# Expert weights into the slot that falls free next, the first pair's rows by gather, scaled rows stored by GpSimd

## The chip, the cores and the metric

One Trainium2 chip; the kernel runs on 1 core of it. The metric is the device time of one execution in microseconds (us). A core has TensorE (PE; its weight loads are listed apart as PEld), VectorE (DVE), ScalarE (ACT), GpSimd (POOL) and SyncE (SP), which here only issues DMAs; 16 DMA engines move the data.

## The reference

One encoder block on 512 tokens of 1024 features, float32. First a mixer (a bidirectional recurrence and a windowed attention, gated and projected), whose result is added to x; then a mixture of experts, the part this case is about, cut from the reference:

```python
g_sel = jnp.argmax(g_logits, axis=-1)
e_in_group = jnp.take_along_axis(e_logits, g_sel[:, None, None], axis=1)[:, 0]
top_val, top_idx = lax.top_k(e_in_group, TOP_K_IN_GROUP)
weights = p_group * jax.nn.softmax(top_val, axis=-1)
...
for e in range(N_EXPERTS):
    he = jax.nn.silu(ht @ w_gate_e[e]) * (ht @ w_up_e[e])
    y = y + combine[:, e:e + 1] * (he @ w_down_e[e])
```

Every token goes to 2 of 32 experts, two of the eight of its group. An expert has a gate and an up matrix of 1024 x 256 and a down matrix of 256 x 1024. The input of the experts is RMSNorm(x1) with the gain `norm2_g`, x1 being the mixer's result.

## The kernel before, in words

The mixer takes the first 630 us or so. What the change touches begins with `out_rows`: the last projection of the mixer gives x1 in four row tiles of 128 tokens, in two column halves. For each of the eight blocks `post` adds x, stores it to the output, transposes it for the router's logits, and lets GpSimd multiply it by the gain `g2` into a tile `r_xg` (two buffers), which SP stores to `h2` in DRAM. `route` then finds each token's two experts on VectorE (one-hot rows `E`, their sum `ES`), counts places with TensorE (`pp`), and builds a list of 64 slots per expert: `pos`, then `r_P`, then 16 small matmuls into the bank `list`, then `idx` (row numbers) for the gathers. The weights of the list (`r_tw`, `r_Pf`, `wgt`, `wts`) and `eid`, for the rare overflow, follow with low priority.

The experts are worked in pairs: pair p is the experts p and p + 16, 64 slots each, side by side on TensorE's columns. For pair 0 the rows are not gathered: `first_x` builds them before `idx` is known, as a product of x1 with a one-hot matrix `r_oh`, in two halves of 16 matmuls (two trace rows each), scaled by `g8` on the way out. For the pairs 1 to 15, `gather` fetches the rows from `h2` by an indirect DMA on GpSimd's queue into one of two tiles `xe`, and `expert_x` transposes them on TensorE into `xT`. `gate_up` is G: 16 matmuls per pair, the first half with the matrices j = 0 of both experts, the second with j = 1. `down` is Y (tile `Yd`), the down product; `finish` scatters it with an add into the output. The loop runs G of pair p, with a piece of the down work of pair p - 1 in its middle, then the transposes of pair p + 1, then Y of pair p - 1. So TensorE is done with the down matrices of pair p - 1 after the gate/up matrices of pair p.

Weights: 96 loads of 1 MB in the order of `USE`: per pair four gate/up pieces (in_wgu) and two down matrices (in_wd). There are 23 slots (`NSLOT`). Load i goes to slot i for i under 23, and then to the slot that load i - 23 had. All loads are issued by SP, which works its queue in order and stands where a slot isn't free. Slots 0 to 14 open during `out_gated` and `out_rows`; slots 15 to 22 lie where the tiles of the output projection and of `route` were (pools `opw`, `op`, and the raw weights), and are free when these are done. In the order of `USE` load 6p + n belongs to pair p; n = 0 to 3 are gate/up, 4 and 5 down.

Of the kernel before, what the change touches and what calls it, by code (L numbers as in the profile page):

```python
# [8 lines left out]
F32 = mybir.dt.float32  # L9
# [3 lines left out]
AF = mybir.ActivationFunctionType  # L13
OP = mybir.AluOpType
# [158 lines left out]


USE = [(p, j, e2) for p in range(16) for j in range(3) for e2 in range(2)]


class K:
# [797 lines left out]
    def out_rows(self):  # L976

        nc, op, zT = self.nc, self.op, self.zT
        x1 = self.x1 = []

        op.tile([P, 4, P], F32, name="x1T", tag="x1T", bufs=2)
        for tt in range(4):
            x1.append(op.tile([P, D], F32, name="x1_%d" % tt))
            nc.sync.dma_start(x1[-1], self.A["x"][tt * P:(tt + 1) * P])
        rl = self.bank("lg", [P, 4, 36], 1)
        ss = op.tile([P, 2, 4], F32, name="r_ss")

        def post(n, tt, ps):

            x = x1[tt][:, n * T:(n + 1) * T]  # L990
            self.tt(x, ps, x, OP.add)
            sl = slice(tt * P, (tt + 1) * P), slice(n * T, (n + 1) * T)
            nc.sync.dma_start(self.A["out"][sl], x)
            self.act(ps, x, AF.Square, scale=1.0 / 32, accum_out=ss[:, n, tt:tt + 1])
            if n + tt == 0:

                self.act(op.tile([P, 1], F32, name="r_tab"), ss[:, 0, 0:1], AF.Sqrt)
            pt = self.bank("mm", [P, 4, P], 4) if n == 1 and tt >= 2 else self.bank("tp", [P, 4, P], 2)
            for k in range(4):
                self.tr(pt[:, k], x[:, k * P:(k + 1) * P])  # L1000
            xT = op.tile([P, 4, P], F32, name="x1T", tag="x1T", bufs=2)
            if n == 1 and tt == 3:
                nc.vector.tensor_copy(xT[:, 0:2], pt[:, 0:2])
                self.act(xT[:, 2:4], pt[:, 2:4])
            elif tt % 2 == 1:
                self.act(xT, pt)
            else:
                nc.vector.tensor_copy(xT, pt)
            for k in range(4):
                self.mm(rl[:, tt], xT[:, k], self.wr[:, 4 * n + k], start=(n + tt + k == 0), stop=(n == 1 and tt + k == 6),  # L1010
                        skip_group_check=True)
            xg = op.tile([P, T], F32, name="r_xg", tag="r_xg", bufs=2)
            self.tt(xg, x, self.g2[:, sl[1]], eng=nc.gpsimd)
            nc.sync.dma_start(self.h2[sl], xg)

        for n in range(2):
            ps = [self.bank("mm", [P, T], 4) for tt in range(4)]
            w = {}
            for m2 in range(4):
                with self.low(-LOW):  # L1020
                    hi, lo = [w_.rearrange("p (a k) b -> p a (k b)", a=2) for w_ in self.wload(4 * n + m2, "w_out")]
                for i in range(2):
                    w[2 * m2 + i] = hi[:, i], lo[:, i]

                ms = [2 * m2, 2 * m2 + 1] if n == 0 or m2 < 2 else range(4, 8) if m2 == 3 else []
                steps = [(m, tt) for m in ms for tt in range(4)]
                for m, tt in sorted(steps, key=lambda u: u[::-1]) if len(ms) == 4 else steps:
                    sl = slice(tt * P, (tt + 1) * P)
                    self.mm3(ps[tt], tuple(t[:, m % 4, sl] for t in zT[m // 4]), w[m], m == 0, m == 7)
                    if m == 7 and tt >= LAG:  # L1030
                        post(n, tt - LAG, ps[tt - LAG])
                self.load_upto(min(NS1 + NS2, NL1 + (NS1 + NS2 - NL1) * (4 * n + m2 + 1) // NL2))
            for tt in range(4 - LAG, 4):
                post(n, tt, ps[tt])
        st = self.st
        self.stt(st, ss[:, 0], 1e-6, ss[:, 1], OP.add, OP.add)
        self.act(st, st, AF.Sqrt)
        nc.vector.reciprocal(st, st)
        lg = op.tile([P, 4, 36], F32, name="r_lg")
        self.tt(lg, rl, st[:, :, None].to_broadcast([P, 4, 36]))  # L1040
        self.tt(lg, lg, self.br[:, None].to_broadcast([P, 4, 36]), OP.add)
        self.route(lg)


    def route_setup(self):
# [9 lines left out]
        nc.sync.dma_start(self.br, bc(self.A["br"], 0, 36))  # L1055
        self.g2 = op.tile([P, D], F32, name="g2")
        nc.sync.dma_start(self.g2, bc(self.A["norm2_g"], 0, D))
        self.g8 = self.rt.tile([P, 8], F32, name="g8")
        nc.sync.dma_start(self.g8, self.A["norm2_g"].rearrange("o (p k) -> p (o k)", p=P))
        self.h2 = self.dram.tile([T, D], F32, name="h2")  # L1060
        rt = self.rt

# [9 lines left out]
    def route(self, lg):  # L1072
# [33 lines left out]
        self.mm(pp, self.tri, ES, start=True, stop=False, skip_group_check=True)  # L1106
        for j in range(3):
            self.mm(pp[:, j + 1:], self.one, bc(ES[:, j, None], 3 - j, 32), start=False, stop=(j == 2), skip_group_check=True)

        m = t1("r_m", 4, 2)  # L1110
        self.stt(m, ES[:, :, ::16], 1e6, pp[:, :, ::16], OP.mult, OP.add)
        oh = self.op.tile([P, 8, 64], F32, name="r_oh", tag="r_xg", bufs=2)
        ready = nc.vector.scalar_tensor_tensor(oh, self.cs("iota")[:, None, :].to_broadcast([P, 8, 64]), 1e6,
                                               m.rearrange("p t h -> p (t h)")[:, :, None].to_broadcast([P, 8, 64]), op0=OP.add, op1=OP.is_equal)
        oh = oh.rearrange("p (t h) s -> p t (h s)", t=4)
        self.first_x(oh, 0)
        tw = self.op.tile([P, 2, 4, 32], F16, name="r_tt")
        self.tt(tw, E, bc(self.cs("tok")[:, None, :, None], 2, 4, 32))
        pos = self.pos
        sc = t3("r_sc")  # L1120
        self.tt(sc, E, bc(pp[:, None], 2, 4, 32))
        with self.tc.issue_after(ready.ins):
            nc.vector.tensor_reduce(pos, sc, axis=V, op=OP.add)
        Pm = self.op.tile([P, 2, 4, 64], F16, name="r_P", tag="x1T", bufs=2)
        self.tt(Pm, bc(self.cs("iota")[:, None, None, :], 2, 4, 64), bc(pos[:, :, :, None], 2, 4, 64), OP.is_equal)
        kt = [(k, i) for k in range(2) for i in range(4)]
        for k, i in kt:
            for h in range(2):
# [1 line left out]
                        stop=(k + i == 4), skip_group_check=True)  # L1130
        self.idx = self.rt.tile([P, 16], I32, name="idx")
        self.slots(self.idx, self.lps[:, 0, :16])
        self.first_x(oh, 1)

        with self.low(), self.tc.issue_after(ready.ins):
            Pf = self.op.tile([P, 2, 4, 64], F32, name="r_Pf", tag="r_xg", bufs=2)
# [22 lines left out]
            sc = self.op.tile([P, 2, 4, 32], F32, name="r_es", tag="r_xg", bufs=2)  # L1159
            self.tt(sc, E, bc(self.cs("iota")[:, None, None, :32], 2, 4, 32))  # L1160
            nc.vector.tensor_reduce(self.eid, sc, axis=V, op=OP.add)

    def first_x(self, oh, hf):

        ps = self.bank("mm", [P, 4, P], 4)
        for k in range(4):
            for tt in range(4):
                self.mm(ps[:, k], self.x1[tt][:, hf * 4 + k:D:8], oh[:, tt], start=(tt == 0), stop=(tt == 3), skip_group_check=True)
        for k in range(4):
            o, g = self.xT[0][:, 4 * hf + k], self.g8[:, 4 * hf + k:4 * hf + k + 1]  # L1170
            if k % 2:
                self.act(o, ps[:, k], AF.Copy, scale=g)
            else:
                self.ts(o, ps[:, k], g)

    def slots(self, idx, ps):

# [93 lines left out]
    def load_upto(self, n):  # L1271

        while self.loaded < min(n, 96):
            p, j, e2 = USE[self.loaded]
            i = self.loaded
            self.slot.append(i if i < NSLOT else self.slot[i - NSLOT])
            self.loaded += 1
            if p == 15 and j == 2:

                for h in range(2 * e2):  # L1280
                    for k in range(2):
                        self.load(i - 1 + k, p, j, k, h)
            else:
                self.load(i, p, j, e2)
# [64 lines left out]
    def moe(self):  # L1349
# [5 lines left out]
            return bass.IndirectOffsetOnAxis(ap=idx, axis=0)  # L1355

        def gather(p):
            xe = xb[(p - 1) % NX]
            if p <= NX:
                nc.gpsimd.memset(xe, 0.0)  # L1360
            nc.gpsimd.indirect_dma_start(out=xe, out_offset=None, in_=self.h2[:, :], in_offset=rows(self.idx[:, p:p + 1]),
                                         bounds_check=T - 1, oob_is_err=False)
            return xe

        def mat(p, j, e2):
            return self.wslot[self.slot[USE.index((p, j, e2))]]
# [4 lines left out]
            self.load_upto(6 * (p + 1) + 4 + NSLOT)  # L1371
            self.scatter(y, self.idx[:, p:p + 1])

        xe = [gather(p) for p in range(1, NX)]
        xT = self.xT[0]
        self.xT.append(self.mo.tile([P, 8, P], F32, name="xT1"))
        self.xn = 0
        for p in range(16):
            if p + NX < 16:
                xe.append(gather(p + NX))  # L1380
            if p == 15:

                for _ in late:
                    pass
                late = None
            sg = self.gate_up([[mat(p, j, e2) for j in range(2)] for e2 in range(2)], xT, self.wts[:, 1, p:p + 1], late)
            if p == 1:
                tasks = self.tasks()
            if p in (1, 4):
                next(tasks)  # L1390
            if p < 15:
                xT = self.expert_x(xe.pop(0))
            for _ in late or ():
                pass
            late = finish(p, sg)
# [75 lines left out]
```

## Time and profile before

| | |
|---|---|
| median of 3 runs | 943.88 us (940.36 to 944.55) |
| the profiled execution | 947.55 us |
| its span, first to last instruction | 945.4 us |
| mean granted TensorE clock | 0.959 |
| PE busy | 829.0 us, 88% of the span |
| PEld busy | 540.2 us, 57% |
| DVE busy | 433.2 us, 46% |
| ACT busy | 309.4 us, 33% |
| POOL busy | 175.8 us, 19% |
| loads of gate/up pieces by SP, issue to landing | 64, median 20.9 us |
| gathers by POOL, issue to landing | 15, median 9.0 us |

Busy shares are means over stages with different limits. The expert part, from some 694 us to the end, is a quarter of the span; what a change there is worth is read from its own stretches and waits. A DMA's issue on SP is shown as a short instruction; when its bytes arrive is its landing. The DMA share is the mean busy share of the 16 DMA engines.

### The profile page before, as it was taken

The numbers are of one execution on the slowest core, as the hardware profiler recorded it, in microseconds if no ns is written. First come the engines' busy times: TensorE is split into PE (matmuls) and PEld (weight loads), VectorE is DVE, ScalarE is ACT, GpSimd is POOL, SyncE is SP. The second block draws the span as 40 slices with busy tenths as digits, with TensorE's granted clock in tenths as the row PEclk, the third lists the DMA queues.
The fourth block names the chain that finished last, engine by engine and source line by source line (L and its number), as shares of the span: only waits on it lengthen the run. The fifth ranks groups of instructions, "written<-read, shape, count | busy, mean of one in ns | idle before, by whom it ended". The sixth has DMA issues, their size and how long they took to land. (4 is left out here: it accounts for less than half of the span.)

```text
span 945.4 us, 17389 instructions
## 1 busy us (share of the span) xinstructions
PE 829.0 (88%) x7248; PEld 540.2 (57%) x7248; DVE 433.2 (46%) x875; ACT 309.4 (33%) x670; POOL 175.8 (19%) x152
## 2 busy tenths in 40 slices
PE   8999887889988987699998999999799998888884
PEld 7676655656666655466666678778653333332221
DVE  5699884565689588124347306632512111111010
ACT  6444531213443553135647522232211111111110
POOL 2611121120003132132313220012111222111101
PEclk9999896999998998699999999999799999999998
DMA  6321131121122322321314648889976999999992
GB/s 220 102 64 38 35 100 37 55 68 57 46 69 77 103 68 68 116 84 59 112 47 139 201 140 317 282 313 364 362 310 245 389 365 394 393 395 404 402 354 49
DMA packets 49775, 175.96 MB, mean 186 GB/s; under 512 B 7639, under 2 KB 14423, under 8 KB 37664
## 3 DMA queue, kind: packets, MB, share of 16 engines
q1 hardware_dynamic: 45232, 166.66, 48.0%
q0 software_dynamic: 4464, 8.18, 3.5%
q8 instruction: 57, 0.93, 0.4%
q14 instruction: 22, 0.18, 0.1%
HBM read 158.78 MB, written 24.12 MB: 193 GB/s over the span
## 5 line engine op out<-in xcount | busy, mean ns | idle before, releaser
L199 PE MATMUL G<-ws,xT 128*64 128x512 f32 x512 | 129.5, 596 | 8.8 <-DMA ws<-in_wgu 5.6
L199 PE MATMUL mm<-hT_hi,w_lo 128*128 128x512 f32 x264 | 114.2, 433 | 7.9 <-ACT oth L184 6.8
L187 POOL TENSOR_TENSOR w_lo<-w_raw,w_hi 128x1024 fp32r<-128x1024 f32 x29 | 70.7, 2438 | 242.9 <-ACT w_hi L184 242.9
L199 PE MATMUL mm<-hT_hi,w_hi 128*128 128x512 f32 x264 | 112.2, 425 | 0.0
L199 PE MATMUL mm<-hT_lo,w_hi 128*128 128x512 f32 x264 | 111.9, 424 | 0.0
L199 PEld LDWEIGHTS G<-ws,xT 128*64 128x64 f32 x512 | 42.8, 137 | 84.3 <-issue 64.4
L199 PE MATMUL Yd<-ws,hT 128*64 128x512 f32 x256 | 67.1, 607 | 10.5 <-ACT y L184 9.4
L184 ACT ACTIVATE w_hi<-w_raw 128x1024 fp32r<-128x1024 f32 x59 | 62.2, 1054 | 28.1 <-PE mm L199 27.9
L199 PEld LDWEIGHTS mm<-hT_hi,w_lo 128*128 128x128 f32 x264 | 52.1, 197 | 25.9 <-issue 14.9
L187 DVE TENSOR_TENSOR w_lo<-w_raw,w_hi 128x1024 fp32r<-128x1024 f32 x30 | 37.1, 1236 | 50.5 <-ACT w_hi L184 50.5
L199 PEld LDWEIGHTS mm<-hT_lo,w_hi 128*128 128x128 f32 x264 | 52.0, 197 | 12.6 <-issue 2.0
L199 PEld LDWEIGHTS mm<-hT_hi,w_hi 128*128 128x128 f32 x264 | 52.2, 198 | 11.5 <-issue 1.7
L187 DVE TENSOR_TENSOR sg<-sg,G 128x256 f32<-128x256 f32 x16 | 6.7, 420 | 100.1 <-ACT sg L184 100.0
L1401 POOL DMA_INDIRECT out<-y,idx x16 | 25.2, 1578 | 127.2 <-DVE y L194 83.1
L194 DVE TENSOR_SCALAR y<-Yd,wts 128x512 f32<-128x512 f32 (+1 forms) x16 | 11.7, 734 | 79.3 <-PE Yd L199 64.8
L184 ACT ACTIVATE sg<-G,wts 128x256 f32<-128x256 f32 x16 | 7.6, 474 | 121.2 <-PE G L199 121.2
L199 PE MATMUL c<-R,T 128*32 128x64 f32 (+1 forms) x992 | 36.3, 231 | 8.2 <-DVE R L647 2.6
L647 DVE COPY R<-c 32x128 f32<-32x128 f32 x64 | 18.8, 293 | 54.0 <-ACT R L184 53.3
L199 PEld LDWEIGHTS Yd<-ws,hT 128*64 128x64 f32 x256 | 17.1, 136 | 45.2 <-ACT y L184 22.4
L199 PE MATMUL tp<-T,KB 64*64 64x128 f32 x512 | 35.6, 284 | 7.4 <-ACT T L184 7.1
L199 PEld LDWEIGHTS c<-R,T 128*32 128x32 f32 (+1 forms) x992 | 26.2, 125 | 27.5 <-issue 13.9
L184 ACT ACTIVATE T<-tp 64x256 f32<-64x256 f32 x64 | 23.9, 377 | 46.1 <-DVE T L187 45.2
(318 smaller groups left out, 1493.0 us busy)
## 6 DMA issues: line engine op xcount, KB each, us to landing
ws<-in_wgu SPq DMA_DIRECT2D x64, 1024.0 KB, 20.9
ws<-in_wd SPq DMA_DIRECT2D x30, 1024.0 KB, 22.3
w_raw<-in_w_in SPq DMA_DIRECT2D x43, 512.0 KB, 3.6
d_oth<-oth SPq DMA_DIRECT2D x16, 256.0 KB, 2.0
w_raw<-in_wo SPq DMA_DIRECT2D x8, 512.0 KB, 4.1
w_raw<-in_w_out SPq DMA_DIRECT2D x8, 512.0 KB, 5.0
x_in<-in_x SPq DMA_DIRECT2D x4, 512.0 KB, 4.8
ga<-d_oth SPq DMA_DIRECT2D x8, 256.0 KB, 5.3
```

What stands on the lines that cost most here:

```text
L184: self.nc.scalar.activation(out, in_, func, **kw)
L187: (eng or self.nc.vector).tensor_tensor(out, a, b, op=op)
L194: self.nc.vector.tensor_scalar(out, a, s1, None, op0=op0)
L199: return self.nc.tensor.matmul(out, l, r, start=start, stop=stop, **kw)
L647: self.nc.vector.tensor_copy(R[u, :, blk, p2], ps[u, 2:4])
L1401: self.nc.gpsimd.indirect_dma_start(out=self.A["out"], out_offset=bass.IndirectOffsetOnAxis(ap=idx, axis=0), in_=y, in_offset=None, bounds ...
```

## The change

Three edits. First, the slot of load i from 23 on is that of the load whose matrix TensorE finishes next, by a table `FREE`: the four gate/up pieces of pair p, then the two down matrices of pair p - 1. Second, `first_x` with `r_m`, `r_oh` and `g8` is gone; pair 0 is gathered and transposed like the others, and the gather of pair 1 is issued after that of pair 0. Third, the eight stores of `r_xg` to `h2` are issued by GpSimd instead of SP. The part of the diff that matters:

```diff
 USE = [(p, j, e2) for p in range(16) for j in range(3) for e2 in range(2)]
+FREE = [i for p in range(17) for i in list(range(6 * p, 6 * p + 4)) + ([6 * p - 2, 6 * p - 1] if p else []) if i < 96]
...
             self.tt(xg, x, self.g2[:, sl[1]], eng=nc.gpsimd)
-            nc.sync.dma_start(self.h2[sl], xg)
+            nc.gpsimd.dma_start(self.h2[sl], xg)
...
-        m = t1("r_m", 4, 2)
-        self.stt(m, ES[:, :, ::16], 1e6, pp[:, :, ::16], OP.mult, OP.add)
-        oh = self.op.tile([P, 8, 64], F32, name="r_oh", tag="r_xg", bufs=2)
-        ready = nc.vector.scalar_tensor_tensor(oh, self.cs("iota")[:, None, :].to_broadcast([P, 8, 64]), 1e6,
...
-        self.first_x(oh, 0)
...
-        with self.tc.issue_after(ready.ins):
-            nc.vector.tensor_reduce(pos, sc, axis=V, op=OP.add)
+        nc.vector.tensor_reduce(pos, sc, axis=V, op=OP.add)
...
-        self.first_x(oh, 1)
...
-            self.slot.append(i if i < NSLOT else self.slot[i - NSLOT])
+            self.slot.append(i if i < NSLOT else self.slot[FREE[i - NSLOT]])
...
-            xe = xb[(p - 1) % NX]
-            if p <= NX:
+            xe = xb[p % NX]
+            if p < NX:
                 nc.gpsimd.memset(xe, 0.0)
...
-        xe = [gather(p) for p in range(1, NX)]
-        xT = self.xT[0]
...
+        x0, last = gather(0)
+        with self.tc.issue_after(last.ins):
+            xe = [gather(1)[0]]
+        xT = self.expert_x(x0)
```

How the instructions move. SP's queue from load 21 on (`ws` is the slot, counted from 0), before:

```order
L1290 DMA ws21_6700<-in_wgu 128x2048
L1290 DMA ws22_6699<-in_wd 128x2048
L1290 DMA ws0_5707<-in_wd 128x2048
L1290 DMA ws1_5708<-in_wgu 128x2048
L1290 DMA ws2_5709<-in_wgu 128x2048
L1290 DMA ws3_5710<-in_wgu 128x2048
L1290 DMA ws4_5711<-in_wgu 128x2048
L1290 DMA ws5_5712<-in_wd 128x2048
L1290 DMA ws6_5713<-in_wd 128x2048
L1290 DMA ws7_5714<-in_wgu 128x2048
```

And the same stretch of SP's queue in the change:

```order
L1269 DMA ws21_6652<-in_wgu 128x2048
L1269 DMA ws22_6651<-in_wd 128x2048
L1269 DMA ws0_5707<-in_wd 128x2048
L1269 DMA ws1_5708<-in_wgu 128x2048
L1269 DMA ws2_5709<-in_wgu 128x2048
L1269 DMA ws3_5710<-in_wgu 128x2048
L1269 DMA ws6_5713<-in_wgu 128x2048
L1269 DMA ws7_5714<-in_wd 128x2048
L1269 DMA ws8_6123<-in_wd 128x2048
L1269 DMA ws9_6124<-in_wgu 128x2048
L1269 DMA ws4_5711<-in_wgu 128x2048
L1269 DMA ws5_5712<-in_wgu 128x2048
```

The down slots 4 and 5 of pair 0 moved behind the gate/up slots 6 to 9 of pair 1.

VectorE in `route`, from `r_P` (the places as one-hot rows) to `idx` and `eid`, in the change:

```order
L1118 TENSOR_TENSOR r_P_6585<-cst_61,pos_5865 128x512
L191 TENSOR_TENSOR r_ge_6607<-r_lg_6545,r_gm_6548 128x16
L191 TENSOR_TENSOR r_ex_6612<-r_mx_6558 128x4
L191 TENSOR_TENSOR r_tw_6619<-r_E_6572,r_st_5863 128x4x32 x2
L191 TENSOR_TENSOR r_es_6640<-r_E_6572,cst_61 128x256
L198 TENSOR_SCALAR idx_6603<-list_5867 128x16
L1153 TENSOR_REDUCE eid_5864<-r_es_6640 128x8
```

Before, `r_es` and `eid` stood behind `idx` and behind the copies out of `first_x`; now `r_es`, which uses a buffer of the tag `r_xg`, stands ahead of `idx`.

GpSimd's queue at the end of `out_rows` and the start of the experts, in the change:

```order
L191 TENSOR_TENSOR r_xg_6475<-x1_0_6135,g2_5855 128x512
L1018 DMA h2_5857<-r_xg_6475 128x512
L191 TENSOR_TENSOR r_xg_6504<-x1_1_6137,g2_5855 128x512
L1018 DMA h2_5857<-r_xg_6504 128x512
L191 TENSOR_TENSOR r_xg_6521<-x1_2_6139,g2_5855 128x512
L1018 DMA h2_5857<-r_xg_6521 128x512
L191 TENSOR_TENSOR r_xg_6539<-x1_3_6141,g2_5855 128x512
L1018 DMA h2_5857<-r_xg_6539 128x512
L1339 MEMSET xe0_6677 128x1024
L1340 DMA xe0_6677<-h2_5857,idx_6603 128x1024
L1339 MEMSET xe1_6678 128x1024
L1340 DMA xe1_6678<-h2_5857,idx_6603 128x1024
```

Before, the eight products stood there without the stores, which were on SP's queue, and the first gather in the queue was that of pair 1; now it is that of pair 0, ahead of the second memset.

## Rows read from the trace of the kernel before

**Rows 1.** Stretches of the span: us, busy us (count) by engine, PEclk, DMA share, GB/s

```profile
690.00:698.00 8.00, 7.05 (x61) 4.53 (x62) 1.46 (x5) 0.73 (x2) 0.00 (x0) 1.00 0.46 158
698.00:702.00 4.00, 4.00 (x22) 1.48 (x19) 0.00 (x0) 0.35 (x1) 0.00 (x0) 1.00 0.86 301
710.00:722.00 12.00, 11.23 (x53) 3.77 (x49) 4.17 (x20) 1.76 (x3) 2.60 (x2) 1.00 0.34 108
722.00:740.00 18.00, 18.00 (x85) 6.94 (x84) 2.14 (x4) 3.09 (x7) 2.64 (x2) 1.00 1.02 385
820.00:910.00 90.00, 74.71 (x314) 27.62 (x311) 10.07 (x16) 10.60 (x20) 12.58 (x9) 1.00 1.01 404
```

**Rows 2.** Waits of PEld after 820 us: us in total, times, longest us

```profile
PEld G L199 <- DMA ws<-in_wgu: 13.5, 12, 2.3
PEld Yd L199 <- DMA ws<-in_wd: 1.2, 3, 0.6
```

**Rows 3.** Waits of SP's queue from 600 us: us in total, times, longest us

```profile
SPq L1290 <- PE Yd L199: 37.4, 5, 16.2
SPq L1290 <- DVE eid L1161: 20.3, 1, 20.3
SPq L1014 <- POOL r_xg L187: 12.7, 6, 5.6
```

**Rows 4.** SP in order of time: start us, us, what it issues

```profile
668.75 0.33 SPq L1014 DMA_DIRECT2D h<-r_xg  x1
670.84 3.17 SPq L1290 DMA_DIRECT2D ws<-in_wgu  x4
694.47 3.99 SPq L1290 DMA_DIRECT2D ws<-in_wd  x2
698.56 20.38 SPq L1290 DMA_DIRECT2D ws<-in_wgu  x4
```

**Rows 5.** Line 1290 between 697 and 698.5 us: duration ns, first and last start

```profile
L1290 SPq DMA_DIRECT2D ws<-in_wd x1: 328/328/328, 698.1 to 698.1; - x1
```

**Rows 6.** TensorE in order of time: start us, us

```profile
676.31 7.92 PE L199 MATMUL mm<-r_oh,x 128*128 128x128 f32 x32 [1.19 <-DVE r_oh L1113]
684.51 7.94 PE L199 MATMUL mm<-r_oh,x 128*128 128x128 f32 x32
694.46 7.09 PE L199 MATMUL G<-ws,xT 128*64 128x512 f32 x32 [0.95 <-ACT xT L184]
701.48 1.15 PE L1301 MATMUL tp<-cst,xe 128*128 128x128 f32 x8
703.96 3.65 PE L199 MATMUL G<-ws,xT 128*64 128x512 f32 x16 [1.34 <-ACT xT L184]
```

**Rows 7.** GpSimd in order of time: start us, us, idle before

```profile
657.14 1.29 POOL L187 TENSOR_TENSOR r_xg<-x,g 128x512 f32<-128x512 f32 x1 [10.01 <-DVE x L187]
666.12 2.60 POOL L187 TENSOR_TENSOR r_xg<-x,g 128x512 f32<-128x512 f32 x2 [6.07 <-DMA h<-r_xg]
685.82 1.23 POOL L1361 DMA_INDIRECT xe<-h,idx  x1 [0.17 <-POOL xe L1360]
```

**Rows 8.** Line 1014, the eight stores of `r_xg` on SP: issue to landing

```profile
DMA to landing us min/median/max: 6.0/6.7/7.5
```

**Rows 9.** Line 1361, the fifteen gathers on GpSimd: issue to landing

```profile
DMA to landing us min/median/max: 8.1/9.0/10.9
```

**Rows 10.** ScalarE's copy of transposed rows, in order of time

```profile
703.32 0.59 ACT L184 ACTIVATE xT<-tp 128x512 f32<-128x512 f32 x1
```

**Rows 11.** Stretches around `first_x`, columns as in rows 1

```profile
670.00:678.00 8.00, 2.14 (x11) 2.01 (x12) 7.21 (x30) 0.79 (x3) 0.95 (x1) 0.50 1.00 355
678.00:680.00 2.00, 2.00 (x10) 2.00 (x10) 1.16 (x6) 0.15 (x2) 0.00 (x0) 0.54 1.02 430
```

**Rows 12.** VectorE in order of time: start us, us

```profile
676.66 0.68 DVE L187 TENSOR_TENSOR r_P<-cst,pos 128x512 f16<-128x512 f32 x1
677.26 0.48 DVE L187 TENSOR_TENSOR r_tw<-r_E,r_st 128x128 f32<-128x128 f16 x2
```

More of the change, by code (lines that the diff above doesn't have):

```diff
@@ L978, in out_rows @@
         nc, op, zT = self.nc, self.op, self.zT
-        x1 = self.x1 = []
+        x1 = []
         op.tile([P, 4, P], F32, name="x1T", tag="x1T", bufs=2)
@@ L1057, in route_setup @@
         nc.sync.dma_start(self.g2, bc(self.A["norm2_g"], 0, D))
-        self.g8 = self.rt.tile([P, 8], F32, name="g8")
-        nc.sync.dma_start(self.g8, self.A["norm2_g"].rearrange("o (p k) -> p (o k)", p=P))
         self.h2 = self.dram.tile([T, D], F32, name="h2")
@@ L1108, in route @@
             self.mm(pp[:, j + 1:], self.one, bc(ES[:, j, None], 3 - j, 32), start=False, stop=(j == 2), skip_group_check=True)
-        m = t1("r_m", 4, 2)
-        self.stt(m, ES[:, :, ::16], 1e6, pp[:, :, ::16], OP.mult, OP.add)
-        oh = self.op.tile([P, 8, 64], F32, name="r_oh", tag="r_xg", bufs=2)
-        ready = nc.vector.scalar_tensor_tensor(oh, self.cs("iota")[:, None, :].to_broadcast([P, 8, 64]), 1e6,
-                                               m.rearrange("p t h -> p (t h)")[:, :, None].to_broadcast([P, 8, 64]), op0=OP.add, op1=OP.is_equal)
-        oh = oh.rearrange("p (t h) s -> p t (h s)", t=4)
-        self.first_x(oh, 0)
         tw = self.op.tile([P, 2, 4, 32], F16, name="r_tt")
@@ L1121, in route @@
         self.tt(sc, E, bc(pp[:, None], 2, 4, 32))
-        with self.tc.issue_after(ready.ins):
-            nc.vector.tensor_reduce(pos, sc, axis=V, op=OP.add)
+        nc.vector.tensor_reduce(pos, sc, axis=V, op=OP.add)
         Pm = self.op.tile([P, 2, 4, 64], F16, name="r_P", tag="x1T", bufs=2)
-        self.tt(Pm, bc(self.cs("iota")[:, None, None, :], 2, 4, 64), bc(pos[:, :, :, None], 2, 4, 64), OP.is_equal)
+        ready = nc.vector.tensor_tensor(Pm, bc(self.cs("iota")[:, None, None, :], 2, 4, 64), bc(pos[:, :, :, None], 2, 4, 64), op=OP.is_equal)
         kt = [(k, i) for k in range(2) for i in range(4)]
@@ L1161, in route @@
             nc.vector.tensor_reduce(self.eid, sc, axis=V, op=OP.add)
[L1163 to L1174, printed above, removed]
     def slots(self, idx, ps):
@@ L1357, in gather @@
         def gather(p):
-            xe = xb[(p - 1) % NX]
-            if p <= NX:
+            xe = xb[p % NX]
+            if p < NX:
                 nc.gpsimd.memset(xe, 0.0)
-            nc.gpsimd.indirect_dma_start(out=xe, out_offset=None, in_=self.h2[:, :], in_offset=rows(self.idx[:, p:p + 1]),
-                                         bounds_check=T - 1, oob_is_err=False)
-            return xe
+            last = nc.gpsimd.indirect_dma_start(out=xe, out_offset=None, in_=self.h2[:, :], in_offset=rows(self.idx[:, p:p + 1]),
+                                                bounds_check=T - 1, oob_is_err=False)
+            return xe, last
         def mat(p, j, e2):
@@ L1372, in finish @@
             self.scatter(y, self.idx[:, p:p + 1])
-        xe = [gather(p) for p in range(1, NX)]
-        xT = self.xT[0]
         self.xT.append(self.mo.tile([P, 8, P], F32, name="xT1"))
         self.xn = 0
+        x0, last = gather(0)
+        with self.tc.issue_after(last.ins):
+            xe = [gather(1)[0]]
+        xT = self.expert_x(x0)
         for p in range(16):
             if p + NX < 16:
-                xe.append(gather(p + NX))
+                xe.append(gather(p + NX)[0])
             if p == 15:
```

## The prediction, made before the result was known

> **What bounds the kernel now.** I read the stretch table first, for the DMA share, because the expert part moves 96 loads of 1 MB each. From 722 us to about 910 us the DMA engines are full (share 1.01 to 1.02), but before that they run empty twice: share 0.46 from 690 to 698 us and 0.34 from 710 to 722 us [rows 1]. Idle DMA time is the share's complement times the length: 0.54 x 8 = 4.3 us, 0.14 x 4 = 0.6 us, 0.66 x 12 = 7.9 us. Whether that time can be won back depends on who is late at the end. The waits of TensorE's weight loads say: after 820 us it stood 13.5 us in 12 places for gate/up slots and 1.2 us for down slots [rows 2]. So the end is set by the loads, and what fills the two holes moves the end, until those 14.7 us are used up.
>
> Then the queue that issues the loads. SP stood 20.3 us once for VectorE's `eid`, and 37.4 us in all, up to 16.2 us at a time, for TensorE's down products [rows 3]. Load 21 (counted from 0 in the order of USE) is issued at 674.0 us; load 22 only at 694.5 us; load 23 at 698.1 us [rows 5]; of the next four the last waits until 718.9 us [rows 4]. TensorE's order tells why [rows 6]. Loads 23 to 26 take the slots of the first pair's gate/up matrices. The first pair's G runs from 694.46 us for 7.09 us, so slots 0 and 1 fall free at half of it, 698.0 us, which is when load 23 goes. Load 27 takes slot 4, a down matrix, which TensorE reads only after the second pair's G; slots 6 and 7 have been free since half of that G, 703.96 + 3.65 = 707.6 us. That is the second hole. The first is load 22: it lies on the routing tiles, whose last use, `eid`, waits for the buffer of `r_oh`, which the second half of `first_x` still reads (TensorE until 692.45 us).
>
> **Part 1, the slots.** Load 27 now takes slot 6, free at G(1)'s half, 9.5 us after load 23. A load of 1.05 MB at 404 GB/s [rows 1] takes 2.6 us, so loads 23 to 26 keep the engines for 10.4 us and load 27 comes in time. Loads 29 and 30 (slots 8, 9) are free 13.5 us after load 23, with work queued until 15.6 us; loads 31 and 32, the down slots, at some 20 us, with work until 20.8 us. From there TensorE only runs ahead of the loads: later it waits for them [rows 2]. The hole of 710 to 722 us goes: **7.9 us**. The 0.6 us of ramp behind load 23 stays. No instruction is added; SP's loads only change address.
>
> **Part 2, the first pair.** `first_x` goes: 7.92 + 7.94 us of TensorE [rows 6], `r_oh` and eight copies. Instead come one gather, eight transposes (1.15 us of TensorE [rows 6]) and two copies. Since `r_oh` is gone, `eid` no longer waits for `first_x`; load 22 can go about 5 us after the last store of the scaled rows, before 691 us, when the engines would run dry. But load 23 hangs on G(0), and G(0) now on this chain: last store landed, `r_es`, `idx`, gather, transposes, copy. In the new order of VectorE `r_es` stands ahead of `idx` and writes a buffer that the last store still reads; the gather waits for all stores anyway. So nothing of this is hidden.
>
> **Part 3, the stores on GpSimd.** SP loses eight issues and the 12.7 us it stood for the products [rows 3]. Nobody gains by that: what stands behind them is loads 15 to 21, which finish earlier and then wait for G(0) all the same. GpSimd gets eight issues. Their price is not in the trace; gathers there take 1.23 us at most of those shown [rows 7], and I take 1.0 us. GpSimd stands idle ahead of the products (6.07 us before the last two [rows 7]), so the issues cost only where product follows product. From issue to landing, X, is the unknown that matters. SP's stores took 6.0 to 7.5 us [rows 8]; gathers from GpSimd's queue, of about the same size and beside the same loads, 8.1 to 10.9 us, median 9.0 [rows 9]. I take 9.0: same engine, same queue.
>
> The Trainium skill, "DMA: Bandwidth & Descriptors", section "Anatomy of one DMA — SWDGE (gpsimd) path", gives such a transfer about 2.0 us plus its bytes at 436 GB/s, an estimate of 2.6 us for these 256 KB; its section "Issuing engine by pattern" puts plain stores on SP. By that figure the stores would not be waited for, and the total would be that of rival (a). Beside full engines the gathers take three times as long [rows 9], so the trace does not agree.
>
> The chain in numbers, from the products' starts [rows 7]: fifth product 657.14 to 658.43, its store lands at 658.43 + X; sixth 659.45 to 660.8, its store 660.8 + X. The two buffers make the seventh wait for the fifth's store: it ends at 658.43 + X + 1.3, 1.0 us of issue follows, and the eighth ends at about 662.15 + X. Its store lands at 662.15 + 2X = **680.2 us** (today it is issued at 668.75 us [rows 4]). Then 0.75 us for `r_es`, `idx` and start, 9.0 us of gather, 1.75 us for four transposes, ScalarE's copy (0.59 us [rows 10]) and the step to TensorE: G(0) starts at 691.7 us. Its half takes 3.55 us at full clock. TensorE has little to do from 670 us on, 2.14 of 8 us: the granted clock is 0.50, 1.2 GHz, from 670 to 678 us and still 0.54 from 678 to 680 us, a rise at about 679.8 us, though `first_x` began at 676.31 us [rows 11]. So G(0) begins at 1.2 GHz. Bounds: nothing, or 3.55 us if the whole half runs so. With a return as slow as behind `first_x` (some 3.5 us), of which transposes and copy take 1.75 us, half of the other 1.75 us is lost, and 0.3 us on the transposes: 1.2 us. Load 23 then goes at 691.7 + 3.55 + 1.2 = 696.4 us instead of 698.1: **1.7 us** won. In short, load 23 goes at 678.4 + 2X.
>
> There is a floor: the list itself. `r_P` starts at 676.66 us today and `r_tw` takes 0.48 us twice [rows 12]; without `r_m` and `r_oh` they come 0.6 us sooner, with `r_es` behind them: `idx` not before about 678.6 us, load 23 not before 694.2 us.
>
> **Sum.** 7.9 + 1.7 = 9.6 us, less than TensorE's 14.7 us of waits, so the loads still set the end. The profiled execution took 947.55 us (span 945.4), so it would take 937.95 us. The median of the runs shown, 943.88 us, is 3.7 us below it; taken off that, **934.3 us**.
>
> **Bounds.** Best: floor, gather in 8.1 us, no clock loss: load 23 at 692.1 us, 6.0 + 7.9 = 13.9 us won, 930.0 us. Worst within the rows: stores and gather at 10.9 us, load 23 at 678.4 + 21.8 + 1.9 = 702.1 us: 7.9 - 4.0 = 3.9 us won, 940.0 us. The three runs lie 4 us apart, which adds 1 to 2 us.
>
> **Rivals.**
> (a) *The early chain is quicker*: stores land as from SP (7 us), so the floor holds: 7.9 + 3.9 = 11.8 us, 932.1 us. For it: loads 15 to 21 and the stores no longer share one queue. Against: the gathers [rows 9].
> (b) *The hole is filled and the end does not move*, because TensorE is the bound: only the 1.7 us stay, 942.2 us. For it: from 722 to 740 us TensorE is busy all the time [rows 1]. Against: 14.7 us of waits later [rows 2].
> (c) *VectorE delays the stores.* From 670 to 678 us it is busy 7.21 of 8 us [rows 11], just when the last store is issued. If that store's work begins only when this stretch ends, 677.6 us, it lands at 686.6 us, load 23 goes at 702.9 us, and 7.9 - 4.8 = 3.1 us stay: 940.8 us. The Trainium skill, "SBUF — State Buffer", section "SBUF: two separate sides", states this as a trap: GpSimd writes a software DMA's descriptors and is locked out while certain VectorE copies run. By that rule the sum is the one just given. No run here shows it; the section "Who interferes with whom" exempts most of the forms that run there.
> (d) *The stores land late and decide*: slower. X counts twice, since the eighth product waits for the sixth's store and the gather for the eighth's. From X = 13.9 us on, load 23 is 7.9 us late and all is lost; at X = 18 us it goes at 714.4 us, 16.3 - 7.9 = 8.4 us worse, 952.3 us. For it: a quarter MB beside up to eight queued MB. Against: no gather took over 10.9 us [rows 9].
>
> **How the numbers follow.** Forecast 0.65, (a) 0.13, (b) 0.08, (c) 0.07, (d) 0.07. What a measurement here can tell from no change is about 0.5%, 4.7 us: faster is below 939.2 us, slower above 948.6 us. Faster holds (a) and 0.62 of the forecast: 0.75. The rest of the forecast, (b) and (c) are within: 0.18. Slower: 0.07. The range reaches from the best bound less half a microsecond, 929.5, to just above (c), 941.5 us; (b) and (d) are left out, as are the forecast's own tails.
>
> **What would show it.** Right: SP issues load 22 before 690 us, load 23 at about 696 us and load 27 without a wait of over 10 us for a down product; the DMA share between 705 and 722 us is near 1; TensorE's waits for slots after 820 us shrink to some 5 us. G(0) starts at 690 to 693 us, the first of its products slow. Wrong: the gather of the first pair starts after 684 us, which is X; or the share is full and TensorE's last products are no earlier, which is (b); or a new hole opens behind load 23.

## The result, and the profile after

| | before | changed |
|---|---|---|
| median of 4 runs each | 942.12 us (940.05 to 944.55) | 930.02 us (928.31 to 931.2) |
| profiled execution, its span | 947.55 us, 945.4 us | 931.2 us, 929.4 us |
| TensorE's matmul of the places (`tp<-ES,tri_h`) starts | 674.68 us | 670.13 us |
| load 23 issued | 698.1 us | 689.7 us |
| from load 23 to the end of the span | 247.3 us | 239.7 us |

The ratio is 0.9869 [0.9834, 0.9904] (in brackets its 95% interval, here and below): faster by 12.3 us of 942.1. The forecast was 934.3 us and the range 929.5 to 941.5 us, so the time lies inside, at its low end; it is near rival (a), 932.1 us.

The two profiled spans differ by 16.0 us, more than the medians. Part of that is no work of the change: a load of `w_in` (line 287 before, 291 after), long ahead of everything the diff touches, is issued at 503.61 us in the profile before and at 500.12 us in the one after, and the matmul of the places comes 4.6 us apart. So positions are compared here from that matmul on, not from the start; before, it is

```profile
674.68 0.29 PE L199 MATMUL tp<-ES,tri_h 128*128 128x128 f16 x1 [5.66 <-DVE ES L187]
```

This shift goes with the execution: over the twelve profiles of this case the matmul starts between 668.3 and 677.3 us. Less what each profiled run lies above the median of its kernel, it is between 668.9 and 672.0 us, and no later with `first_x` (669.0 to 671.0 us) than without. Load 23 comes 23.4 us behind it before and 19.6 us after, 3.8 us sooner; from load 23 to the end is 7.6 us shorter. Together that is 11.4 us, near the 12.3 us of the ratio.

The stretches of the changed kernel, columns as in [rows 1]:

```profile
676.00:684.00 8.00, 2.91 (x37) 2.84 (x38) 0.34 (x2) 0.00 (x0) 1.18 (x2) 0.50 1.01 417
684.00:686.00 2.00, 2.00 (x9) 1.05 (x9) 0.69 (x1) 1.79 (x2) 0.77 (x1) 0.50 0.73 299
686.00:688.00 2.00, 2.00 (x10) 0.55 (x8) 0.00 (x0) 0.09 (x1) 0.22 (x1) 0.68 0.52 117
688.00:690.00 2.00, 2.00 (x12) 0.59 (x10) 0.00 (x0) 0.00 (x0) 0.00 (x0) 1.00 0.22 88
690.00:692.00 2.00, 2.00 (x12) 0.67 (x10) 0.00 (x0) 0.00 (x0) 0.00 (x0) 1.00 0.63 119
710.00:722.00 12.00, 12.00 (x54) 4.28 (x52) 1.11 (x2) 2.14 (x4) 2.65 (x2) 1.00 1.02 400
```

The hole of 710 to 722 us is gone: DMA share 1.02 instead of 0.34 [rows 1]. The hole ahead of load 23 is still there, 684 to 692 us: 0.27 + 0.48 + 0.78 + 0.37 of 2 us each, 3.8 us. The clock stands at 0.50 until 686 us, 1.1 us into G(0), and is at 1.00 from 688 us.

SP in order of time (start us, us, what it issues), and its waits from 600 us (us in total, times, longest us), as in [rows 4] and [rows 3]:

```profile
663.64 2.22 SPq L1269 DMA_DIRECT2D ws<-in_wgu  x4
678.47 11.59 SPq L1269 DMA_DIRECT2D ws<-in_wd  x2
690.16 8.31 SPq L1269 DMA_DIRECT2D ws<-in_wgu  x4
698.57 3.93 SPq L1269 DMA_DIRECT2D ws<-in_wd  x2
```

```profile
SPq L1269 <- PE G L203: 29.2, 9, 10.9
SPq L1269 <- PE Yd L203: 17.7, 4, 6.1
SPq L1269 <- DVE r_tw L191: 10.1, 1, 10.1
```

Load 22 goes at 678.5 us, load 23 at 689.7 us. The four loads behind it take 8.31 us where they took 20.38 us [rows 4]. The wait of 20.3 us for `eid` is one of 10.1 us for `r_tw`; the longest wait for a down product is 6.1 us instead of 16.2 us; and the wait of 10.9 us for G is the one for load 23.

The chain ahead of it, on VectorE, GpSimd and TensorE (start us, us, idle before and its releaser):

```profile
672.77 0.42 DVE L191 TENSOR_TENSOR r_es<-r_E,cst 128x256 f32<-128x256 f16 x1
673.10 0.17 DVE L198 TENSOR_SCALAR idx<-list 128x16 int32<-128x16 f32 x1
```

```profile
659.07 1.26 POOL L191 TENSOR_TENSOR r_xg<-x,g 128x512 f32<-128x512 f32 x1 [3.30 <-DMA h<-r_xg]
660.62 0.57 POOL L1018 DMA_DIRECT2D h<-r_xg  x1 [0.30 <-DMA h<-r_xg]
661.22 1.27 POOL L191 TENSOR_TENSOR r_xg<-x,g 128x512 f32<-128x512 f32 x1
662.79 0.56 POOL L1018 DMA_DIRECT2D h<-r_xg  x1 [0.30 <-POOL r_xg L191]
670.55 0.94 POOL L1339 MEMSET xe<- 128x1024 f32 x1 [7.19 <-PE tp L203]
674.11 1.08 POOL L1340 DMA_INDIRECT xe<-h,idx  x1 [2.62 <-DVE eid L1153]
```

```profile
670.13 0.29 PE L203 MATMUL tp<-ES,tri_h 128*128 128x128 f16 x1 [5.67 <-DVE ES L191]
683.02 1.94 PE L1280 MATMUL tp<-cst,xe 128*128 128x128 f32 x8 [5.00 <-DMA xe<-h,idx]
684.89 8.25 PE L203 MATMUL G<-ws,xT 128*64 128x512 f32 x32
```

From issue to landing, the eight stores on GpSimd, and then its sixteen gathers:

```profile
DMA to landing us min/median/max: 5.3/6.7/8.8
```

```profile
DMA to landing us min/median/max: 4.4/8.7/10.7
```

The stores took 6.7 us in the median, exactly what SP's took [rows 8], not the gathers' 9.0 us [rows 9]. The seventh product did wait for the fifth's store (3.30 us), as forecast, but the last store, issued at 662.79 us, is landed some 7 us later, at about 669.7 us. `idx` is written at 673.10 us, and the gather follows at 674.11 us. So the stores are done over 3 us before the list is: the list decides, which the prediction called the floor.

A price of the third part lies ahead of the matmul of the places, where this comparison does not see it. In the router's chain VectorE's `r_st` runs just when GpSimd makes the eighth product (661.22 us, above):

```profile
660.85 1.67 DVE L194 SCALAR_TENSOR_TENSOR r_st<-r_ss 128x4 f32<-128x4 f32 x1 [0.17 <-ACT mm L188]
```

It ends as the product ends. In a kernel below (late stores), where no product runs beside it, it takes 0.16 us; there `r_E`, 0.42 us in the change, falls beside a product and takes 1.95 us. Before, `r_st` fell beside the seventh product and ended with it, after 0.84 us; the store's issue between the two products puts the eighth in its way. From the last transposes of x1 to the matmul of the places it was 10.1 us before, 11.2 us here, 10.4 us in a second profile of the change and 10.1 us with the stores left on SP. Of the 1.1 us, 0.8 us are `r_st`. So counted from those transposes load 23 is 2.7 us sooner here, 4.2 us in the second profile and 3.7 us with the stores on SP. The medians, 930.02 and 931.01 us for the stores on GpSimd and on SP, do not show this price.

TensorE's waits for slots after 820 us (us in total, times, longest us), against the 13.5 us and 1.2 us of [rows 2]:

```profile
PEld G L203 <- DMA ws<-in_wgu: 7.7, 5, 2.1
PEld Yd L203 <- DMA ws<-in_wd: 0.3, 1, 0.3
```

They shrank by 6.7 us and are not used up: the loads still set the end.

### The profile page after: what moved, and what is told of

Same layout as the page of the kernel before. It is cut to its first block, busy times and chain, and to the rows that moved or that the text cites. A ratio compares the mean times of both kernels' runs of the same rounds, so it can differ in the third digit from the quotient of the medians.

```text
span 929.4 us, 17293 instructions
## 1 busy us (share of the span) xinstructions
PE 814.1 (88%) x7192; PEld 529.8 (57%) x7192; DVE 433.4 (47%) x870; ACT 308.9 (33%) x667; POOL 181.5 (20%) x161
## 5 line engine op out<-in xcount | busy, mean ns | idle before, releaser
L1382 POOL DMA_INDIRECT out<-y,idx x16 | 25.2, 1577 | 117.3 <-DVE y L198 100.4
```

What stands on the lines that cost most here:

```text
L1382: self.nc.gpsimd.indirect_dma_start(out=self.A["out"], out_offset=bass.IndirectOffsetOnAxis(ap=idx, axis=0), in_=y, in_offset=None, bounds ...
```

## The experiments

The theory after this look: the slot order gives about 7.9 us behind load 23; the gathered first pair lets load 23 go about 3.9 us sooner, at the time that the list sets; the stores' engine gives nothing. The rivals: the early lead belongs to the stores (they left SP's queue), or the slots' share is not the hole's 7.9 us. Three kernels do one part each, and one does two.

**The slot table alone**, in the kernel before:

```diff
+FREE = [i for p in range(17) for i in list(range(6 * p, 6 * p + 4)) + ([6 * p - 2, 6 * p - 1] if p else []) if i < 96]
...
-            self.slot.append(i if i < NSLOT else self.slot[i - NSLOT])
+            self.slot.append(i if i < NSLOT else self.slot[FREE[i - NSLOT]])
```

> The slot table alone; first_x and SP's stores stay. Theory (slots 7.9 us, the earlier first pair 3.9 us, stores nothing): load 23 still goes when half of G(0) is done, some 29 us after the router's last product, and the hole behind load 26 is gone: 942.1 - 7.9 = 934.2 us. Rival A (the slots give all of it): 930 us. Rival B (the hole is only moved, because SP's queue stands at the next down slot): 942 us.

Measured: 935.68 us against 943.94 us of the kernel before on that chip, ratio 0.991 [0.9881, 0.9939], 8.5 us. SP in order of time, then two stretches and TensorE's G(0):

```profile
693.44 5.69 SPq L1291 DMA_DIRECT2D ws<-in_wd  x2
699.23 9.40 SPq L1291 DMA_DIRECT2D ws<-in_wgu  x4
```

```profile
692.00:694.00 2.00, 1.05 (x20) 0.56 (x18) 0.92 (x4) 0.58 (x2) 0.00 (x0) 0.93 0.04 8
694.00:696.00 2.00, 2.00 (x8) 0.70 (x6) 0.00 (x0) 0.00 (x0) 0.00 (x0) 0.50 0.82 221
```

```profile
693.43 8.78 PE L200 MATMUL G<-ws,xT 128*64 128x512 f32 x32 [0.95 <-ACT xT L185]
```

The four loads behind load 23 take 9.40 us instead of 20.38 us, and load 23, at 698.8 us, is 239.5 us before the end of the span (938.3 us) instead of 247.3 us: 7.8 us from the slots alone. Load 23 itself is not earlier: 25.2 us behind the matmul of the places, against 23.4 us before. The clock is 1.7 us of it: here it fell to 0.50 some 0.3 us into G(0) (0.93 from 692 to 694 us), after an idle time of 0.95 us ahead of G(0), the same as before, and G(0) took 8.78 us instead of 7.09 us [rows 6]; in the profile before it did not fall there.

**The first pair by gather alone**: the change with the slots in turn and the stores on SP again.

```diff
-            nc.gpsimd.dma_start(self.h2[sl], xg)
+            nc.sync.dma_start(self.h2[sl], xg)
...
-            self.slot.append(i if i < NSLOT else self.slot[FREE[i - NSLOT]])
+            self.slot.append(i if i < NSLOT else self.slot[i - NSLOT])
```

> The gather of the first pair alone; slots in turn and stores on SP. Theory: load 23 goes 3 to 4 us sooner and the hole behind load 26 stays as long as before (DMA share some 0.34 over 12 us): 942.1 - 3.9 = 938.2 us. Rival A (the slots give all): 942 us. Rival C (the gather needs the stores off SP's queue): G(0) no earlier than before or later, 942 to 946 us.

Measured: 938.26 us, ratio 0.9943 [0.992, 0.9965], 5.4 us. Its SP:

```profile
679.64 11.48 SPq L1269 DMA_DIRECT2D ws<-in_wd  x2
691.22 19.29 SPq L1269 DMA_DIRECT2D ws<-in_wgu  x4
```

Load 23 (690.8 us) comes 19.1 us behind the matmul of the places, 4.3 us sooner than before; the 19.29 us, the second hole, are there. The lead is the gather's, and needs neither the slots nor the stores on GpSimd.

**The stores on GpSimd alone**, in the kernel before:

```diff
-            nc.sync.dma_start(self.h2[sl], xg)
+            nc.gpsimd.dma_start(self.h2[sl], xg)
```

> The stores on GpSimd alone. Theory: nothing in the early chain waits for them, 942.1 us, within 0.3%; loads 15 to 21 are issued some 4 us sooner and then wait all the same. Rival D (SP's queue was held by the stores and that cost time): 938 us or less.

Measured: 944.31 us, ratio 1.0009 [0.9986, 1.0033]. Load 23 comes 23.4 us behind the matmul of the places, as before. By the interval at most 1.3 us could be won and 3.1 us lost.

**The change with the stores left on SP** (the first line of the second diff alone):

> The change with the stores left on SP. Theory: the list is the floor of the gather's start, SP's stores land in about 7 us like GpSimd's, so the gather starts within 1.5 us of where it starts in the change: 930 to 931.5 us. Rival C: the last store stands in SP's queue behind other issues and lands later than the list; the gather starts 3 us or more later and the time is 933 us or more.

Measured: 931.01 us, ratio 0.9873 [0.9825, 0.9921], the change's own. The gather:

```profile
672.26 1.23 POOL L1340 DMA_INDIRECT xe<-h,idx  x1 [2.54 <-DVE r_es L191]
```

It starts 3.9 us behind the matmul of the places, in the change 4.0 us; load 23 goes 19.7 us behind it, in the change 19.6 us. So the first two parts are the whole gain as far as the times can tell, and their sum agrees with it: 8.5 + 5.4 = 13.9 us apart, 12.0 us together, with intervals of 2 to 5 us to each side.

**Stores that land late.** The last two stores of the changed kernel are made twice on GpSimd's queue, the second behind the landing of the first. The output does not change.

```diff
             nc.gpsimd.dma_start(self.h2[sl], xg)
+            if n == 1 and tt >= 2:
+                nc.gpsimd.dma_start(self.h2[sl], xg)
```

> The changed kernel with its last two stores of scaled rows made twice, the second waiting for the first to land. Theory: these stores have some 3.5 us to spare in the change (landed by 669.7 us, idx at 673.1 us); two more landings of 6.9 us and one product on the chain put the first gather some 10 us later, and load 23 and the end with it: 930 + 9.9 = 940 us. Rival E (the loads in flight cover a later gather): 930 to 932 us.

Measured: 936.84 us, ratio 0.99 [0.9871, 0.9929], against 945.4 us of the kernel before on that chip. GpSimd, then TensorE, in order of time:

```profile
680.18 0.55 POOL L1020 DMA_DIRECT2D h<-r_xg  x1 [6.50 <-DMA h<-r_xg]
688.07 1.08 POOL L1342 DMA_INDIRECT xe<-h,idx  x1 [6.38 <-DVE r_pg L194]
```

```profile
691.76 1.94 PE L1282 MATMUL tp<-cst,xe 128*128 128x128 f32 x8 [0.81 <-DMA xe<-h,idx]
693.63 8.97 PE L203 MATMUL G<-ws,xT 128*64 128x512 f32 x32
```

The expected 940 us did not come. Late stores do hold the gather: `r_es` starts at 686.72 us, when the last store has landed, `idx` behind it at 687.06 us, and the gather 14.7 us behind the matmul of the places, 10.7 us later than in the change, as expected. But load 23 (699.2 us) is only 6.2 us later against that matmul. The step of this expectation that failed is the gather's own time, taken as fixed: the transposes follow 3.7 us behind its issue, in the change 8.9 us. What differs is the load on the DMA engines. In the change the share is 1.01 from 676 to 684 us, while the gather flies; here it is 0.25 from 688 to 692 us:

```profile
688.00:692.00 4.00, 2.16 (x33) 2.09 (x34) 1.17 (x6) 0.00 (x0) 3.07 (x3) 0.50 0.25 61
```

The change itself has a second such case: its gather issued at 685.23 us, beside a share of 0.37 (686.2 to 690.2 us), landed in 4.4 us, its other fifteen, beside shares near 1, in 7.8 to 10.7 us. No run varied the share alone, so the cause is argued from these rows. Either way part of a late start comes back by itself. From load 23 to the end are 239.4 us, in the change 239.7 us: the end follows load 23. On the same chip it is 5.3 us slower than the next kernel, whose load 23 comes 6.6 us sooner behind that matmul.

**TensorE kept busy while the gather flies**: 16 products of the identity with itself, ahead of the first pair's transposes; nothing uses them.

```diff
+        wb = self.bank("tp", [P, P], 2)
+        for _ in range(16):
+            self.mm(wb, self.ident, self.ident)
         xT = self.expert_x(x0)
```

> The changed kernel with 16 idle products of the identity with itself on TensorE between the list and the first transposes, so that TensorE does not stand before G(0). Theory (G(0) at 1.2 GHz costs 1.2 us, the transposes some 0.5 us): G(0) in 7.1 instead of 8.25 us, load 23 1.7 us sooner, 928.3 us. Rival F (the clock is not what made G(0) long, or the products delay the transposes): G(0) still over 8 us, 930 us or more.

Measured: 931.5 us, ratio 0.9853 [0.9828, 0.9878], on the chip where the kernel before takes 945.4 us. The expected 928.3 us did not come; the rival did, that the products delay the transposes:

```profile
677.03 6.18 PE L203 MATMUL tp<-cst 128*128 128x128 f32 x32 [0.28 <-DVE wts L1162]
683.04 1.05 PE L1280 MATMUL tp<-cst,xe 128*128 128x128 f32 x8
```

The transposes took 1.05 us and G(0) 7.09 us, 0.9 and 1.2 us less than in the change. But the products, 6.18 us long, held the transposes up, and load 23 went 19.2 us behind the matmul of the places, between the 19.6 us and 18.8 us of the change's two profiles: nothing is won.

**One more slot**, to see whether the hole ahead of load 23 can be filled and what bounds then. For its room the output tiles `y` of the down product and `hT` have one buffer instead of two:

```diff
-NY = 2
-NSLOT = 23
+NY = 1
+NSLOT = 24
...
-        hT = mo.tile([P, 2, P], F32, name="hT", tag="hT", bufs=2)
+        hT = mo.tile([P, 2, P], F32, name="hT", tag="hT", bufs=1)
```

> The changed kernel with a 24th slot, paid for with one buffer each for y and hT. Theory: the 3.8 us in which the engines still run empty before load 23 take one load of 2.6 us; one load less remains behind G(0): 930 - 2.6 = 927.4 us. Rival G (one buffer for y makes the down products wait for the scatter, 9.8 us to landing): PE waits on the scatter and 932 us or more.

Measured: 943.83 us, ratio 0.9985 [0.9962, 1.0008]: the whole gain is lost, as the rival said. Its waits from 690 us, of TensorE and then of ScalarE:

```profile
PE Yd L203 <- ACT y L188: 26.9, 16, 7.3
...
PEld G L203 <- DMA ws<-in_wgu: 0.7, 3, 0.3
...
ACT y L188 <- DMA out<-y,idx: 41.0, 10, 12.1
```

The first row in the changed kernel, in the same stretch:

```profile
PE Yd L203 <- ACT y L188: 8.7, 11, 0.8
```

The hole is gone (share 0.99 from 660 to 690 us, in the change 0.89), and TensorE waits for gate/up slots only 0.7 us. But it now stands 26.9 us for ScalarE's `y`, which waits 41.0 us for the scatters that still read the one buffer. The clock, 1.00 from 690 us on in the change, is 0.84 from 760 to 800 us and 0.90 from 800 to 840 us. `hT`'s one buffer cost a single wait of 1.6 us; neither buffer was taken away without the slot. A second run had the 16 products as well:

> Both: the 24th slot and the idle products. Theory: the two add, 930 - 2.6 - 1.7 = 925.7 us. Rival H (TensorE becomes the bound): less than 1 us better than the better of the two.

Measured: 945.16 us, ratio 0.9988 [0.9961, 1.0014], with the same wait at 26.7 us. So the sixteen products do not help where `y` is the bound. Whether a slot could be had elsewhere was not tried.

**Eleven products instead of 16**, timed beside the change itself on one chip (the kernel before: 941.8 us):

> The change itself once more, as the measure for the next run on the same chip. The theory (slots 7.9 us, load 23 earlier by 3.9 us, stores nothing): 0.987 of the kernel before; load 23 issued 19.6 us after the matmul of the places on TensorE, and some 239.5 us before the end of the span. The rival that the early lead is half upstream drift of the profiles: load 23 over 21 us behind that matmul in this run.

> The change with 11 identity products ahead of the first pair's transposes instead of 16, so that they end about when the gather lands. They add work that the result does not use. By the theory of the clock (G(0) at 1.2 GHz costs 1.2 us, the transposes 0.8 us) and of the end that follows load 23 one for one: transposes 1.1 us, G(0) 7.1 to 7.5 us, load 23 some 17.7 us behind the matmul of the places, 1.5 to 2 us sooner than in the change, and 0.998 of the change's time. By the rival that 11 products are too few to bring the clock up in time: transposes and G(0) as in the change (1.94 and 8.25 us) and no gain.

Measured: the change 930.67 us, ratio 0.9883 [0.985, 0.9917]; with eleven products 929.62 us, 0.987 [0.9833, 0.9906]. TensorE with eleven products:

```profile
677.10 3.88 PE L203 MATMUL tp<-cst 128*128 128x128 f32 x22 [0.28 <-DVE wts L1162]
681.28 1.15 PE L1280 MATMUL tp<-cst,xe 128*128 128x128 f32 x8 [0.30 <-DMA xe<-h,idx]
682.73 7.09 PE L203 MATMUL G<-ws,xT 128*64 128x512 f32 x32 [0.30 <-ACT xT L188]
```

The transposes now wait for the gather alone, and both they and G(0) run at full clock. Load 23 is the second of the two `in_wd` loads, here and in the change run beside it:

```profile
677.27 9.46 SPq L1269 DMA_DIRECT2D ws<-in_wd  x2
678.07 10.79 SPq L1269 DMA_DIRECT2D ws<-in_wd  x2
```

It comes, at 686.4 us, 17.5 us behind the matmul of the places; in the change run beside it, at 688.5 us, 18.8 us. The 1.3 us agree with 1.05 us between the medians, but the intervals overlap: the trace shows it, the times do not. That run of the change also answers to the rival that its lead was drift: 18.8 us again, not over 21.

From load 23 to the end of the span, in all profiles with 23 slots:

| slots | kernels | us |
|---|---|---|
| in turn | before, stores alone, gather alone | 247.3, 248.5, 245.7 |
| by the table | change, slots alone, stores on SP, late stores, 16 products, 11 products, change again | 239.7, 239.5, 239.4, 239.4, 238.5, 239.3, 239.5 |

## Why the prediction was right, and where its size was off

- **The slots, 7.9 us: right.** The table above shows 7.6 us for the change and 7.8 us for the slot table alone, which measured 8.5 us in time.
- **The end set by the loads: right.** Load 23 to the end is the same within 1.2 us over the seven profiles with the slot table, whose load 23 comes 17.5 to 25.8 us behind the matmul of the places. Rival (b), TensorE as the bound, would have kept 1.7 us; it fell.
- **The early lead, 1.7 us: the mis-sized term.** The step is "I take 9.0: same engine, same queue" for X, from a store's issue to its landing on GpSimd. Measured were 6.7 us in the median, and SP's stores were the nearer row: the same transfer from the same tile, where the gathers differ in kind. With X at 6.7 us the chain "678.4 + 2X" gives 691.8 us, below the floor of the list, 694.2 us; so the floor held. In terms of the matmul of the places the floor was 19.5 us, and load 23 came at 19.6 us. This is rival (a), given 0.13: that the time lies inside the range is owed to the bound that was drawn for the floor, and not to the chain that the forecast took as the one that decides. Of the 4.3 us by which the time lies below the forecast, this term is 2.1 us; 1.8 us are the base, a median of 943.88 us of three runs where the result has 942.12 us of four, and have nothing to do with the mechanism. The issue cost, taken at 1.0 us, was 0.56 us.
- The Trainium skill, "DMA: Bandwidth & Descriptors", section "Anatomy of one DMA — SWDGE (gpsimd) path", gave an estimate of 2.6 us by its formula for this store. The measured 6.7 us do not agree. Yet its consequence, that the gather would not wait for the stores, held, since the list was later still; one product did wait 3.30 us for a store.
- **The clock, 1.2 us: right in sum, not in its parts.** From the start of the transposes to load 23 the change took 6.7 us, its second profile 6.1 us, and the kernel with eleven products, at full clock, 5.1 us: a price of 1.6 and 1.0 us. Taken were 0.3 us on the transposes and 0.9 us on G(0). All eight transposes took 1.94 us, 0.8 us over 1.15 us, and G(0) 8.25 us, 1.2 us over 7.09 us [rows 6], in the second profile 7.63 us. Of the 1.3 us that the eleven products give back, 1.0 us lie behind the start of the transposes.
- **Rival (c)** did not come: VectorE was busy 5.96 of 8 us from 662 to 670 us, and the last store, issued in that stretch, landed in 6.9 us, inside it. Which of VectorE's forms could hold a store was not tested. **Rival (d)** is real as a mechanism (late stores hold the gather) but was 3 us away, and a gather beside emptier engines gives some of the delay back.
- **The hole ahead of load 23**, 4.3 us before, was not priced in the sum. Load 22 went at 678.5 us, while the engines were full; they ran dry from some 685 us until load 23 had gone, 3.8 us of idle time.
- Of the signs, load 22 before 690 us, a share near 1 behind 705 us and no wait of over 10 us for a down product came; TensorE's waits shrank to 8.0 us and not to 5; G(0) and load 23 came earlier than said.
- **Not settled**: why profiled executions differ by 3.5 us already at 500 us, where the programs are alike; and how large the gain of each part is to better than 2 us, since the intervals are that wide.

## What to carry to other kernels

When loads wait for slots, list for each load the moment its slot's last reader ends: one load that waits for a late slot holds every load behind it, and the idle DMA time that follows is what the order can win, as long as the consumers still wait for loads later. For a transfer moved to another queue, take its landing from the same transfer on the old queue rather than from another kind on the new one, and look for the next thing in the chain (here the list) before giving all of its time away. Time a second limit before spending buffers on the first: one more slot paid for with an output buffer cost the whole gain.

## What the runs showed of the hardware

- A plain store of 256 KB from GpSimd landed as soon as one from SP, 6.7 us in the median from either (5.3 to 8.8 us and 6.0 to 7.5 us), beside DMA engines busy 0.95 and 0.92 of the time.
- The same gather was followed by its transposes 8.9 us behind its issue beside engines at a share of 1.01 and 3.7 us beside engines at 0.25.
- Two of VectorE's operations with two inputs in SBUF took 1.67 and 1.95 us while GpSimd issued a store and multiplied two tiles beside them, and 0.16 and 0.42 us where it did not.
- TensorE's clock went to 1.2 GHz (0.50) at the start of G(0) in one profile and not in another, behind the same matmuls and the same idle time of 0.95 us; G(0) took 8.78 us and 7.09 us. With eleven products, 3.88 us, ahead of them the first pair's transposes ran at 2.4 GHz (1.15 us), without them at 1.2 GHz (1.94 us).
